# Attention in one encoder layer: the per-block sums over keys folded from 128 to 64 partitions ahead of their transposes

## The chip, the cores and the metric

The kernel runs on one core of a Trainium2 chip. The metric is the device time of one execution in microseconds (us), the median of the runs shown. The core's engines work side by side, each through its own queue of instructions in a fixed order: TensorE (PE, with its weight loads shown as PEld), VectorE (DVE), ScalarE (ACT), GpSimd (POOL) and SyncE (SP), which here issues DMAs.

## What is computed

One layer of a hybrid encoder over 2048 positions of width 1024. A combined projection feeds two groups of heads: a gated linear attention (chunked, in both directions) and a latent attention with softmax over all 2048 keys. Their outputs are joined, projected by a 1024x1024 matrix, added to the scaled input and normalised. The change lies in the softmax attention, whose core is

```python
s = (jnp.einsum('bqhd,bkhd->bhqk', qn, k_nope) + jnp.einsum('bqhr,bkr->bhqk', qr, k_r))
p = jax.nn.softmax(s, axis=-1)
return jnp.einsum('bhqk,bkhv->bqhv', p, v)
```

for 4 heads. What matters for the change is the denominator of the softmax: for each query, the sum over all keys of exp(s - maximum).

## The kernel before

The program has three long stages one after the other: sweeps over the input that make projections, the linear attention and the latent keys and queries (to about 637 us of the profile), the softmax attention (to about 1100 us, its last block running on into the next stage), and the output projection with the normalisation.

The attention works on 16 blocks, each one head and 512 queries (`blocks`, numbered i from 0 to 15). A block has 8 key steps j, each of two tiles of 128 keys. Scores stand transposed: keys on the 128 partitions, the 512 queries along the row. Every product is done in three passes over high and low halves, so that float32 accuracy is kept. The steps of a block, by their functions:

- `scores` (L1512): ten matmuls of 512 columns into a PSUM tile `pS` of two banks; two such tiles take turns. `copy` (L1526, ACT) brings it to SBUF as `s`, and `smax` (L1531, DVE) keeps a running maximum `rm` from PSUM. A tile `pS` is free for the scores two steps later when both have read it.
- `tmax`, `rmax`, `bmax`: four transposes of `rm` (tile `mx`), a reduction along the row, and four more transposes that broadcast the maximum (`mb`).
- `sub` (DVE), `exp` (ACT), `phi` (ACT) and `plo` (POOL): the exponentials and their high and low halves `ph`, `pl`.
- `pv` (L1600): six matmuls that add the step's part to the block's output `o`.
- `acc0`, `acc`: the sums of the exponentials over the key steps. Steps 0, 1, 2, 5 are added in PSUM (`ap`, one buffer) by DVE, after `acc0` on ACT has started it with a copy; steps 3, 4, 6, 7 are added in SBUF (`as`, shown as `acc`, two rows of 512) by POOL.
- `tot` (L1610): DVE joins the two, so that `as[:, 0]` holds for each partition and each query the sum over the 16 key tiles. What is left is the sum over the 128 partitions.
- `tsum` (L1625): four transposes of 128x128 put queries on partitions (tile `sx`, L1629); `rcp` (L1631) adds along the row (L1635) and takes the reciprocal (L1636). `keep` stores it to DRAM for the output stage.
- `oh`, `ol`, `y`, `yc`: the block's output is split, multiplied by the value weights and stored.

The order of all of this on every engine is written out by hand: each step has a place on a common scale (`PLACE`), whole numbers being the score steps; the steps are sorted by place and each engine's instructions are chained in that order. Block i's `tot` is at 8i + 7 + 11.2, which is within block i+2's scores; by then block i+1 is in its exponentials. The last block (15) follows a table of its own and closes during the output projection; block 14's closing steps run among the first products of the output projection.

Lines that the change and the prediction touch: `tot` L1616 and L1617, `tsum` L1629, `rcp` L1635, `acc0` L1585, `copy` L1529, `smax` L1542, `exp` L1570, the split helper L365 (ACT: `ph`, `ofh`) and L371 (POOL and DVE: `pl`, `ofl`), the scores L1520 to L1524.

Of the kernel before, what the change touches and what calls it, by code (L numbers as in the profile page):

```python
# [12 lines left out]
AF = mybir.ActivationFunctionType  # L13
ALU = mybir.AluOpType
AX = mybir.AxisListType
# [12 lines left out]
QB = 512  # L28
# [56 lines left out]
    rmax=1.27,  # L85
    bmax=1.48,
    tot=11.2,
    tsum=12.04,
    rcp=13.55,
    keep=14.21,  # L90
    oh=12.34,
    ol=12.99,
    y=16.55,
    yc=16.9,
# [260 lines left out]
class K:  # L355
# [1130 lines left out]
    def attention(self):  # L1486
        tc, nc = self.tc, self.nc
        mm = nc.tensor.matmul
        V, G, Ac = nc.vector, nc.gpsimd, nc.scalar
        NP = NKT // 2  # L1490
        with ExitStack() as ctx:
# [6 lines left out]
            nb = len(blocks)  # L1498
            stt = [dict(s=[None] * NP) for _ in blocks]
# [110 lines left out]
            def tot(i):  # L1610
                d = stt[i]
                if i == nb - 1:
                    d["as"] = self.keep.tile([P, 2, QB], F32, tag="acc", name=f"acc{i}")
                    V.tensor_copy(d["as"][:, 0], d["ap"])
                    return
                V.tensor_tensor(d["ap"], d["ap"], d["as"][:, 1], ALU.add)  # L1616
                V.tensor_tensor(d["as"][:, 0], d["ap"], d["as"][:, 0], ALU.add)  # L1617

            def close(i, shape, name, other):


                p, tag = other if i == nb - 1 else (pX, "x")
                return p.tile(shape, F32, tag=tag, name=name)

            def tsum(i):  # L1625
                d = stt[i]
                d["x"] = close(i, [P, 4, P], f"sx{i}", (pA, "ap"))
                for e in range(4):
                    nc.tensor.transpose(d["x"][:, e], d["as"][:, 0, e * P:(e + 1) * P], self.ident)  # L1629

            def rcp(i):  # L1631

                d = stt[i]
                rc = op.sm.tile([P, 4], F32, tag="rc", name=f"rc{i}")
                V.tensor_reduce(rc, d["x"], AX.X, ALU.add)  # L1635
                V.reciprocal(rc, rc)  # L1636
                d["rc"] = rc

# [58 lines left out]
            def at(f, i, j=None):  # L1697
                p = PLACE_LAST.get(f, PLACE[f]) if i == nb - 1 else PLACE[f]
                return p[j] if isinstance(p, tuple) else p

            own = (("tot", tot), ("tsum", tsum), ("rcp", rcp), ("keep", keep), ("oh", oh), ("ol", ol), ("y", y), ("yc", yc))
            own_late = tuple(e for e in own if e[1] is not keep)
            for i in range(nb):
                for j in range(NP):
# [81 lines left out]
            for c in range(4, NCH):  # L1786
                with fixed():
                    split(c + 2)
                    load(c + 4)
                    if 4 < c < NCH - 1:  # L1790
                        op.load_res(rest[c + 1])
                    op.product(rest[c])
                    op.finish(rest[c])
                with self.after(*last.values()), fixed():
                    if c == 4:
                        keep(nb - 2)
                    for f in {4: (tot, oh, ol), 5: (tsum, rcp), 7: (turn, y, rows, yc)}.get(c, ()):
                        f(nb - 1)
# [212 lines left out]
```

## Time and profile before

| what | us |
|---|---|
| median of 3 runs (lowest, highest) | 1307.95 (1307.42, 1308.66) |
| the profiled execution | 1308.66 |
| its span, first to last instruction | 1306.3 |
| outside the span | 2.36 |
| TensorE busy in the span | 1280.9 (98%) |
| 637 to 1098 us, the attention: busy PE, POOL, DVE, ACT | 459.1, 407.7, 401.1, 381.2 of 461.0 |
| 1098 to 1145 us: busy PE | 46.0 of 47.0 |
| 1145 to 1306 us, the output projection: busy PE | 150.3 of 161.0 |

Busy time of an engine is the share of the stretch in which one of its instructions ran. Matmuls overlap, so the time that one of them costs is read from the distance between starts, not from its own duration. A line of the timeline gives start, duration from the first start to the last end, engine, line of the code, output and inputs, the count, and in brackets how long the engine had been idle and what released it.

### The profile page before, as it was taken

To read this page: it belongs to the slowest core of one execution; us is meant where nothing else is said; L and a number is where in the kernel's file an instruction comes from. 1 tells how busy PE (TensorE), PEld (TensorE's weight loads), DVE (VectorE), ACT (ScalarE), POOL (GpSimd) and SP (SyncE) were. 2 spreads that over 40 slices of the span, in tenths; PEclk is the share of its full clock that TensorE was granted. 3 is DMA by queue.
4 is the path that set the end of the run, shared out by engine and by line. 5 is a ranking of instruction groups with operands and counts; after the bars stand their busy time and mean duration, and the time that the engine had idled before them with its cause. 6 is when DMAs were issued, how large, how long until landed. Compare 5 with 4: busy or idle time off the path is not lost.

```text
span 1306.3 us, 19979 instructions
## 1 busy us (share of the span) xinstructions
PE 1280.9 (98%) x7081; PEld 1130.9 (87%) x7081; DVE 958.2 (73%) x1712; ACT 812.8 (62%) x1339; POOL 783.6 (60%) x494
## 2 busy tenths in 40 slices
PE   7999999999999999999999999999999999999997
PEld 7999999999989999999788888888888887887786
DVE  6967774645675455555798888888888888377998
ACT  6764656655575656655688878888888888411110
POOL 0143333242457666672298888889999999934441
PEclk9999999999999999999999999999999999999999
DMA  8131313122475565565501111122123110376563
GB/s 285 61 101 54 94 49 91 55 68 79 132 249 170 193 214 181 178 210 170 145 1 41 41 42 41 41 57 65 58 81 97 41 41 12 119 234 175 195 197 109
DMA packets 107820, 145.81 MB, mean 112 GB/s; under 512 B 17251, under 2 KB 62695, under 8 KB 107721
## 3 DMA queue, kind: packets, MB, share of 16 engines
q1 hardware_dynamic: 99128, 142.41, 35.6%
q0 software_dynamic: 672, 2.10, 0.4%
q8 instruction: 56, 0.92, 0.3%
q10 hardware_dynamic: 7920, 0.03, 0.3%
q14 instruction: 44, 0.35, 0.2%
HBM read 94.14 MB, written 50.36 MB: 111 GB/s over the span
## 4 chain that ended last, share of the span: by engine, by line
PE 83%; DMA 4%; DVE 3%; ACT 2%; POOL 1%; issue 1%; SPq 1%; DVEq 0%; POOLq 0%; ACTq 0%
PE pS L1520 4%; PE o L419 4%; PE o L420 4%; PE o L421 4%; PE pS L1522 4%; PE pS L1523 4%; PE pS L1521 4%; PE pS L1524 4%; PE ipa L419 4%; PE ipa L421 4%; PE ipa L420 4%; PE pz L420 2%; PE pz L419 2%; PE pz L421 2%; PE ipg L419 2%; PE ipg L420 2%
## 5 line engine op out<-in xcount | busy, mean ns | idle before, releaser
L371 POOL TENSOR_TENSOR pl<-s,ph 128x1024 fp32r<-128x1024 f32 x128 | 306.5, 2414 | 58.3 <-ACT ph L365 54.5
L1542 DVE TENSOR_TENSOR rm<-pS,rm 128x512 f32<-128x512 f32 x210 | 144.8, 690 | 36.5 <-ACT s L1529 31.2
L1529 ACT ACTIVATE s<-pS 128x1024 f32<-128x1024 f32 x128 | 131.4, 1027 | 60.6 <-PE pS L1524 51.3
L1566 DVE TENSOR_TENSOR s<-s,mb 128x1024 f32<-128x1024 f32 x128 | 151.2, 1213 | 9.5 <-PE mb L1560 9.3
L1029 POOL TENSOR_TENSOR Us<-Us,cw 128x512 f32<-128x512 f32 x16 | 18.5, 1157 | 227.2 <-DVE Us L1027 175.3
L365 ACT ACTIVATE ph<-s 128x1024 fp32r<-128x1024 f32 x128 | 135.2, 1057 | 17.1 <-PE o L421 16.5
L1570 ACT ACTIVATE s<-s 128x1024 f32<-128x1024 f32 x128 | 131.4, 1050 | 13.7 <-DVE s L1566 13.7
L419 PE MATMUL ipa<-wah,xah 128*128 128x384 f32 (+1 forms) x384 | 131.1, 342 | 6.7 <-ACT wah L365 6.7
L421 PE MATMUL ipa<-wah,xal 128*128 128x384 f32 (+1 forms) x384 | 125.5, 327 | 0.0
L420 PE MATMUL ipa<-wal,xah 128*128 128x384 f32 (+1 forms) x384 | 125.2, 326 | 0.0
L1520 PE MATMUL pS<-qh,ckvT_h 128*128 128x512 f32 x256 | 102.6, 401 | 0.8 <-DVE rm L1542 0.4
L419 PE MATMUL o<-ph,vh 128*128 128x512 f32 x256 | 101.0, 395 | 0.0
L421 PE MATMUL o<-ph,vl 128*128 128x512 f32 x256 | 99.8, 390 | 0.0
L1522 PE MATMUL pS<-qh,ckvT_l 128*128 128x512 f32 x256 | 99.8, 390 | 0.0
L1523 PE MATMUL pS<-rh,krs 128*128 128x512 f32 x256 | 99.8, 390 | 0.0
L1524 PE MATMUL pS<-rl,krs 128*128 128x512 f32 x256 | 99.7, 389 | 0.0
L1521 PE MATMUL pS<-ql,ckvT_h 128*128 128x512 f32 x256 | 99.7, 389 | 0.0
L420 PE MATMUL o<-pl,vh 128*128 128x512 f32 x256 | 99.7, 389 | 0.0
L1593 DVE TENSOR_TENSOR ap<-ap,s 128x512 f32<-128x512 f32 x120 | 83.0, 692 | 2.7 <-ACT s L1570 0.7
L371 POOL TENSOR_TENSOR ol<-of,oh 128x512 fp32r<-128x512 f32 x32 | 42.9, 1343 | 66.9 <-ACT oh L365 66.9
L419 PEld LDWEIGHTS ipa<-wah,xah 128*128 128x128 f32 x384 | 73.7, 192 | 7.9 <-ACT wah L365 7.0
L419 PE MATMUL pz<-xch,wzh 128*128 128x256 f32 x256 | 74.8, 292 | 0.0
(325 smaller groups left out, 3858.0 us busy)
## 6 DMA issues: line engine op xcount, KB each, us to landing
xcf<-xT_dram SPq DMA_DIRECT2D x16, 512.0 KB, 4.9
xr<-x_dram SPq DMA_DIRECT2D x16, 512.0 KB, 6.6
out_dram<-rr SPq DMA_DIRECT2D x32, 256.0 KB, 2.0
xaf<-xT_dram SPq DMA_DIRECT2D x14, 512.0 KB, 4.2
oib<-oi_s SPq DMA_DIRECT2D x16, 256.0 KB, 4.4
qdb<-qd_s SPq DMA_DIRECT2D x16, 256.0 KB, 4.6
SU<-su_s SPq DMA_DIRECT2D x16, 256.0 KB, 4.9
ub<-u_s SPq DMA_DIRECT2D x16, 256.0 KB, 4.7
```

The lines of the kernel that those rows point to most:

```text
L365: return nc.scalar.activation(dst, src, AF.Copy).ins
L371: return e.tensor_tensor(dst, src, hi.bitcast(F32), ALU.subtract).ins
L419: mm(out, ah, bh, start=start, stop=False)
L420: mm(out, ah, bl, start=False, stop=False)
L421: mm(out, al, bh, start=False, stop=stop)
L1520: mm(ps[:, e], kh, qh, start=True, stop=False)
L1521: mm(ps[:, e], kh, ql, start=False, stop=False)
L1522: mm(ps[:, e], kl, qh, start=False, stop=False)
L1523: mm(ps[:, e], kr, rh, start=False, stop=False)
L1524: mm(ps[:, e], kr, rl, start=False, stop=True)
L1542: V.tensor_tensor(d["rm"], src[:, e], d["rm"], ALU.max)
L1566: V.tensor_tensor(s, s, d["mb"][:, None, :].to_broadcast([P, 2, QB]), ALU.subtract)
```

## The change

Ahead of the transposes, the 128 partitions are folded to 64. `tot` now leaves the joined sum in PSUM (`ap`). A new step `own_half` on ACT (two copies of 64 partitions by 256 queries) puts partitions 0 to 63 of queries 0 to 255 and partitions 64 to 127 of queries 256 to 511 into `as[:, 0, :256]`. A new step `fold` on DVE (two additions of 64 by 256) adds the other 64 partitions of the same queries, which it reads from PSUM across the partition halves. `as[:, 0, :256]` then holds two sums of 64 partitions for every pair of queries, one above the other, and `tsum` needs two transposes in place of four; `rcp` adds rows of 64 in place of rows of 128. The last block keeps the former way. The places are 11.7 for `own_half`, 11.95 for `fold` and 12.37 for `tsum` (12.04 before).

```diff
     tot=11.2,
-    tsum=12.04,
+    half=11.7,
+    fold=11.95,
+    tsum=12.37,
...
-                V.tensor_tensor(d["ap"], d["ap"], d["as"][:, 1], ALU.add)
-                V.tensor_tensor(d["as"][:, 0], d["ap"], d["as"][:, 0], ALU.add)
+                for e in range(2):
+                    V.tensor_tensor(d["ap"], d["ap"], d["as"][:, e], ALU.add)
+
+            halves = [(slice(64 * e, 64 * e + 64), slice(64 - 64 * e, 128 - 64 * e), slice(e * QB // 2, (e + 1) * QB // 2))
+                      for e in range(2)]
+
+            def own_half(i):
+                d = stt[i]
+                for own_p, _, qs in halves:
+                    Ac.activation(d["as"][own_p, 0, :QB // 2], d["ap"][own_p, qs], AF.Copy)
+
+            def fold(i):
+                d = stt[i]
+                for own_p, other_p, qs in halves:
+                    h = d["as"][own_p, 0, :QB // 2]
+                    V.tensor_tensor(h, d["ap"][other_p, qs], h, ALU.add)
...
-                for e in range(4):
+                for e in range(4 if i == nb - 1 else 2):
                     nc.tensor.transpose(d["x"][:, e], d["as"][:, 0, e * P:(e + 1) * P], self.ident)
...
-                V.tensor_reduce(rc, d["x"], AX.X, ALU.add)
+                if i == nb - 1:
+                    V.tensor_reduce(rc, d["x"], AX.X, ALU.add)
+                else:
+                    V.tensor_reduce(rc.rearrange("p (e j) -> p j e", e=2),
+                                    d["x"][:, 0:2].rearrange("p j (e k) -> p j e k", e=2), AX.X, ALU.add)
...
-            own = (("tot", tot), ("tsum", tsum), ("rcp", rcp), ("keep", keep), ("oh", oh), ("ol", ol), ("y", y), ("yc", yc))
+            own = (("tot", tot), ("half", own_half), ("fold", fold), ("tsum", tsum), ("rcp", rcp), ("keep", keep), ("oh", oh), ("ol", ol), ("y", y), ("yc", yc))
```

What stands in a row on an engine is shown for the end of block 6, which falls into block 8's scores; the other blocks up to 13 read the same. A name's first number in a row, where it has two, is the key step; the last is the program's own count. Here is DVE before, from `tot` to the reduction of `rcp`: `rm` and `pS` belong to block 8, `s` and `mb` to block 7, `acc` to block 6.

```order
L1616 TENSOR_TENSOR ap_9658<-ap_9658,acc_9788 128x512
L1617 TENSOR_TENSOR acc_9788<-ap_9658,acc_9788 128x512
L1542 TENSOR_TENSOR rm_9881<-pS_1_9870,rm_9881 128x512 x2
L1566 TENSOR_TENSOR s_3_9685<-s_3_9685,mb_9857 128x1024
L1542 TENSOR_TENSOR rm_9881<-pS_2_9899,rm_9881 128x512 x2
L1566 TENSOR_TENSOR s_4_9731<-s_4_9731,mb_9857 128x1024
L1566 TENSOR_TENSOR s_5_9760<-s_5_9760,mb_9857 128x1024
L371 TENSOR_TENSOR ofl_9965<-o_9720,ofh_9955 128x512
L1542 TENSOR_TENSOR rm_9881<-pS_3_9935,rm_9881 128x512 x2
L1593 TENSOR_TENSOR ap_9932<-ap_9932,s_0_9592 128x512
L1635 TENSOR_REDUCE rc_10004<-sx_9946 128x4
```

The same stretch of DVE after the change:

```order
L1619 TENSOR_TENSOR ap_9670<-ap_9670,acc_9800 128x512 x2
L1544 TENSOR_TENSOR rm_9893<-pS_1_9882,rm_9893 128x512 x2
L1568 TENSOR_TENSOR s_3_9697<-s_3_9697,mb_9869 128x1024
L1633 TENSOR_TENSOR acc_9800<-ap_9670,acc_9800 64x256 x2
L1544 TENSOR_TENSOR rm_9893<-pS_2_9911,rm_9893 128x512 x2
L1568 TENSOR_TENSOR s_4_9743<-s_4_9743,mb_9869 128x1024
L1568 TENSOR_TENSOR s_5_9772<-s_5_9772,mb_9869 128x1024
L373 TENSOR_TENSOR ofl_9979<-o_9732,ofh_9966 128x512
L1544 TENSOR_TENSOR rm_9893<-pS_3_9951,rm_9893 128x512 x2
L1595 TENSOR_TENSOR ap_9946<-ap_9946,s_0_9602 128x512
L1654 TENSOR_REDUCE rc_10018<-sx_9968 128x2x2
```

Nothing changes its place; the two additions of `fold` are put in between a `sub` of block 7 and the maximum of block 8's step 2. On ACT, the copies of `own_half` come between block 7's `ph` of step 0 and block 8's copy of step 2, after the change:

```order
L1572 ACTIVATE s_0_9602<-s_0_9602 128x1024
L367 ACTIVATE ph_0_9934<-s_0_9602 128x1024
L1627 ACTIVATE acc_9800<-ap_9670 64x256 x2
L1531 ACTIVATE s_2_9944<-pS_2_9911 128x1024
L1587 ACTIVATE ap_9946<-s_0_9602 128x512
L1572 ACTIVATE s_1_9633<-s_1_9633 128x1024
L367 ACTIVATE ofh_9966<-o_9732 128x512
L367 ACTIVATE ph_1_9971<-s_1_9633 128x1024
L1531 ACTIVATE s_3_9975<-pS_3_9951 128x1024
```

Before, the same rows stood there without the third; `ap_9946` is block 7's `acc0`, which writes the single buffer `ap` that `fold` reads two rows of work earlier. On PE the transposes `sx` stay between block 8's scores of step 3 and of step 4, two in place of four.

## The prediction

> **What bounds the kernel now.** I read the head of the page first, then the attention's stretches by engine, then PE's timeline around the transposes that the change halves. All these rows are of the kernel before; the first pair is from the page, the third from the table of stretches (PE, PEld, DVE, ACT, POOL busy, then granted clock, DMA share and GB/s) for one period of the attention, from the end of block 6's sum to the end of block 7's.
>
> ```profile
> span 1306.3 us, 19979 instructions
> PE 1280.9 (98%) x7081; PEld 1130.9 (87%) x7081; DVE 958.2 (73%) x1712; ACT 812.8 (62%) x1339; POOL 783.6 (60%) x494
> ...
> 858.77:889.89 31.12, 31.12 (x145) 25.79 (x144) 27.00 (x38) 26.18 (x29) 27.65 (x12) 1.00 0.03 9
> ```
>
> PE is busy for all of the 31.12 us at the full granted clock, while DVE, ACT and POOL have 3.5 to 5 us free in each period. A busy PE may still be a slow one, so the spacing of its matmuls is what counts. PE's timeline, with the scores of block 8 around block 6's transposes:
>
> ```profile
> 864.39 0.39 PE L1524 MATMUL pS<-rl,krs 128*128 128x512 f32 x1
> 864.62 0.60 PE L1629 MATMUL sx<-ident,acc 128*128 128x128 f32 x4
> 864.98 0.48 PE L1520 MATMUL pS<-qh,ckvT_h 128*128 128x512 f32 x1
> 865.29 0.39 PE L1521 MATMUL pS<-ql,ckvT_h 128*128 128x512 f32 x1
> ...
> 868.70 0.39 PE L1520 MATMUL pS<-qh,ckvT_h 128*128 128x512 f32 x1
> 870.97 0.39 PE L419 MATMUL o<-ph,vh 128*128 128x512 f32 x1
> ```
>
> Matmuls of 512 columns start every 0.23 us (864.39 to 864.62 here), with no gap before the transposes. So in the attention PE's own list of instructions is the time, and whatever is taken from it counts in full, as long as no wait opens.
>
> **What the change takes from PE.** One transpose lasts 272 ns by the group of its line:
>
> ```profile
> L1629 PE MATMUL sx<-ident,acc 128*128 128x128 f32 x64 | 9.6, 272 | 0.0
> ```
>
> Four take 0.60 us from the first start to the last end, so three spacings are 0.60 - 0.272 = 0.328, or 0.109 us each. The whole group costs 864.62 to 865.29 less one ordinary spacing, 0.67 - 0.23 = 0.44 us, four times 0.11: the price is linear in the count. Two transposes less are 0.218 us a block, and 15 of the 16 blocks change: 3.27 us. The bounds from the same rows: if only the way to the next start counts, 0.36 / 4 = 0.09 us a transpose, 2.7 us in all; with the slow matmul behind them spread over the four, 0.11 each, 3.4 us. I take 3.27, since neighbours in a row are what is removed.
>
> The Trainium skill has a lower price: "TensorE: Matmul & The Clock Gate", section "Back-to-back issue gap", gives about 81 ns for a pair of weight load and matmul of 128 columns in a sustained stream. By it the sum would be 30 x 0.081 = 2.4 us, an estimate from that page, which would not be told from no change; the 0.109 us measured here stands against it.
>
> **What the change adds.** Prices by the nearest rows, first ACT then DVE:
>
> ```profile
> L1267 ACT ACTIVATE sqm<-ipm 128x256 f32<-128x256 f32 x16 | 6.1, 384 | 12.6 <-DVE rope L1469 9.6 <-PE ipm L421 3.0
> L365 ACT ACTIVATE qbh<-qd 64x512 fp32r<-64x512 f32 x32 | 20.2, 631 | 8.2 <-DVE qd L936 7.7
> L1465 DVE TENSOR_TENSOR qrf<-pqr,cos 128x256 f32<-128x256 f32 x16 | 6.7, 419 | 5.5 <-PE pqr L421 5.5
> L371 DVE TENSOR_TENSOR qbl<-qd,qbh 64x512 fp32r<-64x512 f32 x32 | 23.6, 737 | 2.9 <-ACT qbh L365 2.3
> ```
>
> 64 partitions of 512 cost as much as full rows of 512 below, so the row length decides, and I take the rows of 256 from PSUM. Neighbours overlap by about 0.1 us, so `own_half` is 2 x 0.384 - 0.1 = 0.67 us of ACT (at most 1.16, by 64x512) and `fold` 2 x 0.419 - 0.1 = 0.74 us of DVE (at most 1.37). `rcp`'s reduction halves its row, 0.68 to about 0.42, and gives 0.26 back. The second addition of `tot` keeps its form and only writes elsewhere. None of it is on PE; the question is whom it makes late. ACT and DVE in the period above, before the change, and POOL's row that follows ACT's `ph` of 863.04:
>
> ```profile
> 858.27 1.06 ACT L365 ACTIVATE ph<-s 128x1024 fp32r<-128x1024 f32 x1
> 859.89 1.03 ACT L1529 ACTIVATE s<-pS 128x1024 f32<-128x1024 f32 x1 [0.56 <-PE pS L1524]
> 860.81 0.59 ACT L1585 ACTIVATE ap<-s 128x512 f32<-128x512 f32 x1
> 861.33 1.05 ACT L1570 ACTIVATE s<-s 128x1024 f32<-128x1024 f32 x1
> 862.55 0.60 ACT L365 ACTIVATE ofh<-o 128x512 fp32r<-128x512 f32 x1 [0.17 <-PE o L421]
> 863.04 1.05 ACT L365 ACTIVATE ph<-s 128x1024 fp32r<-128x1024 f32 x1
> 864.88 1.03 ACT L1529 ACTIVATE s<-pS 128x1024 f32<-128x1024 f32 x1 [0.78 <-PE pS L1524]
> ```
> ```profile
> 858.08 0.69 DVE L1617 TENSOR_TENSOR acc<-ap,acc 128x512 f32<-128x512 f32 x1
> 860.01 1.21 DVE L1566 TENSOR_TENSOR s<-s,mb 128x1024 f32<-128x1024 f32 x1
> 861.14 1.41 DVE L1542 TENSOR_TENSOR rm<-pS,rm 128x512 f32<-128x512 f32 x2
> 865.94 1.42 DVE L1542 TENSOR_TENSOR rm<-pS,rm 128x512 f32<-128x512 f32 x2 [0.53 <-ACT s L1529]
> 867.87 0.68 DVE L1635 TENSOR_REDUCE rc<-sx 128x4 f32<-128x512 f32 x1
> ```
> ```profile
> 864.23 2.41 POOL L371 TENSOR_TENSOR pl<-s,ph 128x1024 fp32r<-128x1024 f32 x1 [2.35 <-ACT ph L365]
> ```
>
> - `own_half` waits for `tot`, done at 858.77, and ACT is free at 859.33 and idle for 0.56 us: the copy behind it moves from 859.89 to about 860.0.
> - `fold` starts where the maximum stood, 861.14, and ends near 861.9. It pushes block 8's step 2 maximum to 861.9 to 863.3. The scores at 864.98 wait for that one; their lead shrinks from 2.4 to 1.7 us.
> - The new wait: `acc0` of block 7 writes `ap`, which `fold` still reads, so ACT stands from 861.0 to 861.9 and `acc0` moves from 860.81 to 861.95. Behind it `exp`, `ofh`, `ph` and the next copy are queued. The idle times 0.17 and 0.78 take 0.95 of the 1.14 us, so the copy of 864.88 comes about 0.2 us late, and so does the maximum of 865.94 (DVE's own 0.74 less its idle 0.53 is also 0.2). The scores at 868.70 reuse that tile: free at 867.36 before, a lead of 1.34 us, now about 1.1. The shorter reduction then makes DVE whole.
> - POOL's `pl` of 864.23 waits for `ph`, about 1 us late, and ends at 867.6 instead of 866.64; the `pv` that reads it starts at 870.97, still 3.3 us later.
> - `sx` itself had 5.85 us from `tot`'s end to 864.62; `fold` ends 2.7 us ahead of it.
>
> With the upper prices `fold` ends at 862.5, `acc0` is 1.7 us late, the copy of 864.88 0.75 and the lead of 868.70 0.5 us; still no wait on PE.
>
> Block 14 closes outside this pattern:
>
> ```profile
> 1107.56 1.21 DVE L1566 TENSOR_TENSOR s<-s,mb 128x1024 f32<-128x1024 f32 x1
> 1107.68 0.60 ACT L1585 ACTIVATE ap<-s 128x512 f32<-128x512 f32 x1 [0.45 <-DVE acc L1617]
> 1111.19 0.60 ACT L365 ACTIVATE ofh<-o 128x512 fp32r<-128x512 f32 x1 [1.92 <-PE o L421]
> 1110.99 0.60 PE L1629 MATMUL sx<-ident,acc 128*128 128x128 f32 x4
> ```
>
> `fold` follows the `sub` and ends near 1109.4, 1.5 us ahead of `sx`; `acc0` slips by 1.8 us into ACT's 1.92 us of idle time. Covered, with little to spare.
>
> **Whether the tail passes it on.** PE is not gapless after the attention. The chain that ended last (start, length, what):
>
> ```profile
> 1142.01 0.03 PE o L421
> 1142.04 3.60 DMA xr<-x_dram
> ...
> 1208.38 0.70 DVE rr L1926
> 1209.08 0.14 issue
> 1209.22 0.47 PE pmb L419
> ```
> ```profile
> 1205.90:1209.67 3.77, 0.62 (x3) 0.44 (x3) 1.25 (x2) 0.00 (x0) 0.05 (x1) 1.00 0.98 307
> 1209.67:1213.08 3.41, 3.41 (x10) 2.62 (x9) 3.31 (x8) 0.92 (x3) 0.47 (x1) 0.50 0.76 237
> ```
>
> PE stands for about 3.2 us until 1209.22, behind a chain of transfers, and then runs 3.41 us at half clock. But that chain was released at 1142.04 by PE itself, by the last block's products. An attention that ends 3.27 us earlier starts the chain as much earlier. So the tail moves along.
>
> **The sum.** 1308.66 - 3.27 = 1305.4 for the profiled execution (2.36 us of it outside the span). The median lies 0.71 below that run: 1304.7, or -0.25%. Changes within 0.2%, 2.6 us, count as no change, about what a measurement of this kernel can tell; so the forecast lies just outside.
>
> **The rivals.**
>
> - *The gain is partly lost.* The tail's stall depends on how transfers fall, and the half clock behind it lasted 3.41 us, in which 10 matmuls took the time of 15: 1.7 us. A longer stall could bring a second such stretch, +1.7, for 1306.4; without any it would be 1303.0. The lowest price of a transpose, 0.09, gives 1305.3. For it: the three runs before already spread over 1.24 us. Against it: the chain's start moves with PE, and the spacing inside the group is plain. The Trainium skill, "TensorE: Matmul & The Clock Gate", section "What's actually happening", says that the clock follows a free-running window of 3413 ns; this trace's 3.41 us agree. By that rule a shift of 3.27 us neither keeps nor removes the half-clock stretch for sure.
> - *Slower: PE waits for ACT at the scores of 868.70.* The place is `acc0` behind `fold`. It decides once ACT is late by more than 0.95 + 1.34 = 2.3 us, against my 1.14; each period then costs PE the excess, 14 times, and from 0.23 us of excess the gain is gone. At an excess of 0.5 us it is +7.0 - 3.27, 1311.7. Against it: even the upper prices reach 1.7. For it: three engines hand on in a row (DVE, ACT, DVE, ACT), and a semaphore hop of 0.14 us, as at 1209.08, stands in each.
> - *Nothing is gained, since weight loads hide transposes.* Then 1307.9; the spacing of 0.109 with a matmul behind each speaks against it, so I give it no chance beside the first rival's.
>
> **How the numbers follow.** Whole saving 0.64 (1304.0 to 1305.3); whole saving and no half-clock stretch 0.05 (near 1303.0); partly lost 0.21 (1305.3 to 1307.5); slower 0.10 (near 1311.7). The predicted time is the first case's. Faster by over 0.2% is 0.64 + 0.05 = 0.69, within it 0.21, slower 0.10. The range 1303.0 to 1306.8 leaves out the slower case and the top of the partly lost one, under 2 in 10; the two prices of a transpose lie inside it.
>
> **What would show it.** Right: `sx` in pairs, about 0.38 us from the first start to the last end; periods of 30.90 us in place of 31.12; no idle time on PE in the attention; `acc0` waiting up to 1 us for DVE; the output's chain starting near 1138.8. Wrong: PE waiting for `rm`, for `fold` or for `pl` in each block; a stall before `pmb` well over 3 us; or a pair of transposes that costs over 0.3 us.

## The result and the profile after

The changed kernel takes 1304.42 us (median of 14 runs, 1302.11 to 1306.13), the kernel before took 1308.14 us beside it (median of 14). The ratio is 0.9972, with a 95% interval from 0.9965 to 0.9979: 0.28% faster, or 3.7 us. The profiled execution of the changed kernel took 1305.11 us, that of before 1308.66. From the head of its page:

```profile
span 1303.1 us, 20008 instructions
PE 1276.8 (98%) x7051; PEld 1126.2 (86%) x7051; DVE 970.7 (74%) x1742; ACT 821.2 (63%) x1369; POOL 783.8 (60%) x494
```

PE has 30 matmuls fewer, DVE and ACT 30 instructions more each. PE's timeline of the changed kernel (start, length, then the operation) at block 6's transposes:

```profile
863.85 0.39 PE L1526 MATMUL pS<-rl,krs 128*128 128x512 f32 x1
864.08 0.38 PE L1645 MATMUL sx<-ident,acc 128*128 128x128 f32 x2
864.22 0.48 PE L1522 MATMUL pS<-qh,ckvT_h 128*128 128x512 f32 x1
864.53 0.39 PE L1523 MATMUL pS<-ql,ckvT_h 128*128 128x512 f32 x1
...
867.73 0.39 PE L423 MATMUL o<-ph,vl 128*128 128x512 f32 x1
867.96 0.39 PE L1522 MATMUL pS<-qh,ckvT_h 128*128 128x512 f32 x1
...
894.96 0.38 PE L1645 MATMUL sx<-ident,acc 128*128 128x128 f32 x2
```

There are pairs now, 0.38 us from the first start to the last end. From the first transpose to the second matmul behind the group it is 0.45 us, where 0.23 would be one ordinary spacing: the pair costs 0.22. The period, from one `sx` to the next, is 894.96 - 864.08 = 30.88 us. Over blocks 0 to 13 it is 30.889 us on average, before 31.102: 0.213 us less. The matmuls before the scores of 867.96 keep their spacing of 0.23, so no gap has opened. PE's waits (what it waited for: us in total, times, longest) in the attention and behind it, of before and then of after, show no new one either (the two lines not shown are the same in both):

```profile
PE pmb L419 <- DVE rr L1926: 3.1, 1, 3.1
PE mx L1548 <- DVE rm L1542: 1.3, 2, 1.0
...
PE pS L1520 <- DVE rm L1542: 0.4, 1, 0.4
```
```profile
PE pmb L421 <- DVE rr L1946: 3.0, 1, 3.0
PE mx L1550 <- DVE rm L1544: 1.0, 2, 0.7
...
PE pS L1522 <- DVE rm L1544: 0.4, 1, 0.4
```

ACT and DVE of the changed kernel in the same period:

```profile
858.69 0.75 ACT L1627 ACTIVATE acc<-ap 64x256 f32<-64x256 f32 x2
859.47 1.03 ACT L1531 ACTIVATE s<-pS 128x1024 f32<-128x1024 f32 x1
861.66 0.60 ACT L1587 ACTIVATE ap<-s 128x512 f32<-128x512 f32 x1 [1.17 <-DVE acc L1633]
...
864.57 1.02 ACT L1531 ACTIVATE s<-pS 128x1024 f32<-128x1024 f32 x1
```
```profile
860.71 0.86 DVE L1633 TENSOR_TENSOR acc<-ap,acc 64x256 f32<-64x256 f32 x2
861.60 1.42 DVE L1544 TENSOR_TENSOR rm<-pS,rm 128x512 f32<-128x512 f32 x2
...
865.79 1.41 DVE L1544 TENSOR_TENSOR rm<-pS,rm 128x512 f32<-128x512 f32 x2
...
867.72 0.41 DVE L1654 TENSOR_REDUCE rc<-sx 128x4 f32<-128x256 f32 x1
```

`acc0` (L1587) now stands 1.17 us for the fold, and ACT's idle time ahead of the copy of 864.57 is gone. The maximum of 865.79 ends at 867.20; the scores that need its tile start at 867.96, a lead of 0.76 us where it was 1.34.

So the time went where the change took it. Followed through the two profiled executions:

| place on PE | before | after | difference |
|---|---|---|---|
| first `sx` (block 0) | 678.00 | 678.74 | +0.74 |
| `sx` of block 13 | 1082.33 | 1080.30 | -2.03 |
| `sx` of block 14 | 1110.99 | 1108.50 | -2.49 |
| `sx` of block 15 | 1182.88 | 1180.15 | -2.73 |
| first `pmb` behind the tail's stall | 1209.22 | 1206.32 | -2.90 |
| span | 1306.3 | 1303.1 | -3.2 |

Of the 0.74 us, 0.69 were there at PE's first wait of the attention (637.90 before, 638.59 after), behind work that the change does not touch; the first `sx` of the other kernels below that have it at this place stands anywhere from 677.50 to 678.32. From block 0 to block 13 the gain is 2.77 us, 13 x 0.213. The rest of the path gives it on and adds a few tenths: the two waits of `mx`, one of which lies between blocks 13 and 14, are 0.3 us shorter in all.

The time outside the span moved as well: 2.36 us in the profiled execution before, 2.0 in that of after and within 0.1 us of it in all 14 runs. It is 2.0 in every kernel below that has the half copy and the fold (1.75 in the one with a second fold), and 2.3 in the two with the transposes alone and in the middle of the 56 runs of the kernel before beside the experiments. So about 0.3 of the 3.7 us lies outside the span, and no run shows what it comes from.

### The profile page after: what moved, and what is told of

It is laid out like the page before. It is cut to its first block, busy times and chain, and to the rows that moved or that the text cites. A ratio compares the mean times of both kernels' runs of the same rounds, so it can differ in the third digit from the quotient of the medians.

```text
span 1303.1 us, 20008 instructions
## 1 busy us (share of the span) xinstructions
PE 1276.8 (98%) x7051; PEld 1126.2 (86%) x7051; DVE 970.7 (74%) x1742; ACT 821.2 (63%) x1369; POOL 783.8 (60%) x494
## 4 chain that ended last, share of the span: by engine, by line
PE 82%; DVE 4%; DMA 4%; ACT 3%; POOL 2%; issue 1%; SPq 0%; DVEq 0%; ACTq 0%; POOLq 0%
PE o L421 4%; PE o L422 4%; PE o L423 4%; PE pS L1522 4%; PE pS L1524 4%; PE pS L1523 4%; PE pS L1525 4%; PE pS L1526 4%; PE ipa L421 4%; PE ipa L423 4%; PE ipa L422 4%; PE pz L422 2%; PE pz L423 2%; PE pz L421 2%; PE ipg L421 2%; PE ipg L422 2%
```

## The experiments

The theory: PE's list of instructions is the time in the attention, each transpose costs it about 0.11 us, and the added half copy and fold lie beside PE's work and use up only margin. The rivals: a transpose's price is hidden or other than that; the added work costs something, and the gain would be larger without it. All were timed in five rounds beside the kernel before, which took 1306.32 us in the first group of four, 1305.62 in the second and 1306.33 in the group of three. The expectations count their absolute times from some 1308 us, so the ratios are what to compare. A period is the average over blocks 0 to 13, as above, and in the first group the middle one of the 13.

**Each half of the change alone, first try.** Of four kernels three held a substitute that I thought neutral: a constant operation of DVE in place of `rcp`'s reciprocal.

```diff
-                V.reciprocal(rc, rc)
+                V.tensor_scalar(rc, rc, 1.0, None, ALU.add)   # blocks 0 to 14
```

Two transposes without the half copy and the fold:

> Two transposes a block in place of four, with neither own_half nor fold (tot as before the change; half of each sum is left out, and blocks 0 to 14 add a constant where the reciprocal stood, one instruction of the same shape). Theory (TensorE's own list is the time, the added work of ScalarE and VectorE is covered): the same as the changed kernel, about 1304.6, pairs of 0.38 us, periods of 30.89 us. Rival (the added work costs part of the gain): 1.5 us or more below the changed kernel, 1303 or less. Rival (the gain comes from elsewhere, the tail for one): close to 1308.

Measured: 1303.42 us, ratio 0.9979 (0.9970 to 0.9988), period 30.91 us. The half copy and fold with all four transposes:

> own_half and fold as in the change, but four transposes and the full reduction (the sums are then wrong, and a constant is added where the reciprocal stood). Theory: the kernel before, 1308.0 within 0.7, periods of 31.1 us, no wait of TensorE in the attention. Rival (the added work costs something that two transposes hide): over 1309.

Measured: 1311.82 us, ratio 1.0045 (1.0032 to 1.0059), period 31.58. One transpose in place of two:

> One transpose a block in place of two (the second 128 queries are left out, the reduction takes four parts of the one; a constant in place of the reciprocal). Theory (0.109 us a transpose, linear down to one): 15 x 0.108 = 1.6 us less than the changed kernel, 1302.8, periods of 30.78 us. Rival (81 ns a transpose): 1303.2. Rival (the last transpose of a group carries the fixed cost of the slow matmul behind it, so that it cannot be saved and nothing is won): 1304.4.

Measured: 1311.33 us, ratio 1.0041 (1.0028 to 1.0053), period 31.58, though PE has less to do than in the changed kernel. Both slow ones wait at the scores one step later than those I had watched, here in the run with one transpose:

```profile
876.01 0.39 PE L423 MATMUL o<-ph,vl 128*128 128x512 f32 x1
876.92 0.47 PE L1522 MATMUL pS<-qh,ckvT_h 128*128 128x512 f32 x1 [0.52 <-DVE rm L1544]
```

The substitute is the cause they share. The rows of DVE and then POOL in the run with one transpose, and the groups of that instruction in the runs with the fold alone and with the pairs alone:

```profile
871.41 1.58 DVE L1658 TENSOR_SCALAR rc<-rc 128x4 f32<-128x4 f32 x1
```
```profile
868.19 4.78 POOL L373 TENSOR_TENSOR pl<-s,ph 128x1024 fp32r<-128x1024 f32 x2 [3.46 <-ACT ph L367]
```
```profile
L1659 DVE TENSOR_SCALAR rc<-rc 128x4 f32<-128x4 f32 x15 | 16.6, 1110 | 0.5
```
```profile
L1659 DVE TENSOR_SCALAR rc<-rc 128x4 f32<-128x4 f32 x15 | 16.4, 1094 | 0.5
```

Four elements a row take 1.1 to 1.6 us in all blocks but the last that has it (0.17), where the reciprocal takes 0.18. So these runs added about 1 us of DVE ahead of the next step's maximum, together with the fold, and they say nothing on the fold by itself. With the pairs alone, where DVE has no fold to do, the same 1.1 us were covered.

**The fold later on DVE.** One number of the order changes, the fold goes behind the maximum of step 2, so that `acc0` waits longer.

```diff
-    fold=11.95,
+    fold=12.25,
```

> Only fold moves, from before block i+2's maximum of step 2 to behind it (place 12.25). Theory: acc0, and with it ScalarE's exp, ofh, ph and copy of step 3, come about 1.3 us later than in the changed kernel, which is 0.5 us more than the lead of the scores that reuse that tile; TensorE waits about 0.4 to 0.5 us for the maximum of step 3 in each of 14 periods: 1310 to 1311.5. Rival (the leads read from the trace are not what decides, or the lateness is taken up elsewhere): no change, about 1304.4.

Measured: 1311.62 us, ratio 1.0047 (1.0035 to 1.006), period 31.58. ACT, DVE and PE of that run, around block 6's close, and PE's wait of the whole run:

```profile
867.00 0.60 ACT L1587 ACTIVATE ap<-s 128x512 f32<-128x512 f32 x1 [2.49 <-DVE acc L1633]
...
869.91 1.02 ACT L1531 ACTIVATE s<-pS 128x1024 f32<-128x1024 f32 x1
```
```profile
866.05 0.85 DVE L1633 TENSOR_TENSOR acc<-ap,acc 64x256 f32<-64x256 f32 x2
...
870.96 1.42 DVE L1544 TENSOR_TENSOR rm<-pS,rm 128x512 f32<-128x512 f32 x2 [1.07 <-ACT s L1531]
```
```profile
871.76 0.39 PE L423 MATMUL o<-ph,vl 128*128 128x512 f32 x1
872.52 0.47 PE L1522 MATMUL pS<-qh,ckvT_h 128*128 128x512 f32 x1 [0.37 <-DVE rm L1544]
```
```profile
PE pS L1522 <- DVE rm L1544: 6.4, 15, 0.9
```

This is the slower rival of the prediction, made to happen: `acc0` waits 2.49 us for the fold in place of 1.17, the copy behind it comes late, DVE waits 1.07 us for the copy, and PE stands for the maximum, once a period (0.76 us from start to start in place of 0.23). The period is 0.69 us longer than the changed kernel's. The wait is 0.53 of it, a little more than the 0.4 to 0.5 expected; the matmul behind the delayed one starts 0.31 us after it in place of 0.23, another 0.08; the last 0.08 are spread over many spacings.

**The halves of the change again, with the reciprocal kept.** Two transposes alone (the reduction reads each of the two tiles twice):

```diff
# in the kernel before
-                for e in range(4):
+                for e in range(4 if i == nb - 1 else 2):
```

> The kernel before with one edit: two transposes a block in place of four, and a reduction that still reads 512 elements, the two tiles twice (the second 256 queries of a block get the first's sums). Reciprocal kept. Theory: 15 x 0.218 = 3.3 us less than the kernel before, as the changed kernel. Rival (the added work of the change costs part of the gain): 4 us or more below the kernel before.

Measured: 1302.58 us, ratio 0.9976 (0.9966 to 0.9985), period 30.888 us. That is the change's own period, 30.889. The half copy and fold with four transposes (of two pieces, each twice):

```diff
# in the changed kernel
-                for e in range(4 if i == nb - 1 else 2):
-                    nc.tensor.transpose(d["x"][:, e], d["as"][:, 0, e * P:(e + 1) * P], self.ident)
+                for e in range(4):
+                    s = e if i == nb - 1 else e % 2
+                    nc.tensor.transpose(d["x"][:, e], d["as"][:, 0, s * P:(s + 1) * P], self.ident)
```

> The changed kernel with four transposes, the two of the change done twice, and a reduction that adds both (a block's sums then come out wrong), reciprocal kept. Theory: the added work is covered, and the slow result of the first attempt came from the constant's addition, which took 1.1 us in place of 0.18: the kernel before within 0.7 us, periods of 31.1 us, no wait of TensorE. Rival (0.26 us more of reduction on VectorE already uncovers a wait): 2.5 us or more above the kernel before.

Measured: 1304.91 us, ratio 0.9997 (0.9987 to 1.0006), period 31.124 us. The reduction in this kernel stayed the changed kernel's short one, so this is the change without its gain on PE and nothing else. And one transpose in place of two, whose tile the reduction reads twice:

> The changed kernel with one transpose a block in place of two; the reduction has the shape of the change and reads the one tile twice (half of the queries get other sums), reciprocal kept. Theory (0.108 us a transpose down to the last but one): 1.6 us below the changed kernel, that is 5.0 below the kernel before, periods of 30.78 us. Rival (81 ns a transpose): 1.2 below the changed kernel. Rival (TensorE, 0.1 us a period faster, meets the maximum of step 3 or 4): periods of 30.9 us or more.

Measured: 1299.96 us, ratio 0.9956 (0.9941 to 0.9971), period 30.788 us, with no new wait on PE.

These three settle the account. The added work alone changes nothing that can be measured; the transposes alone give the change's whole gain of the period (of the time 0.24% in place of 0.28%, within the intervals); a third transpose less gives another step of the same size. By the periods, one transpose is worth (31.124 - 30.889) / 2 = 0.117 us with the fold, (31.102 - 30.888) / 2 = 0.107 without it, and 30.889 - 30.788 = 0.101 from two to one. The first two prices differ because the two kernels with four transposes do, 31.124 and 31.102, with the same list on PE.

**Whose margin it is.** Three more kernels test it. One moves the fold and `acc0`, one `acc0` alone (behind ACT's copy of step 3, where it does not wait for the fold), and one lengthens the reduction. First the late fold with a late `acc0`:

```diff
-    acc0=10.78,
+    acc0=11.75,
-    fold=11.95,
+    fold=12.25,
```

> The late fold of the third experiment, and acc0 behind ScalarE's copy of step 3 (place 11.75; block 15 keeps 10.78), so that exp, ofh, ph and the copy no longer stand behind the wait for fold. Theory (the late fold cost 7 us through acc0's wait alone): the changed kernel's time, periods of 30.89 us, no wait of TensorE. Rival (the late fold costs through VectorE, whose later work it pushes): periods of 31.5 us and some 5 us above the kernel before, as with the late fold.

Measured: 1303.08 us, ratio 0.9979 (0.9969 to 0.9989), period 30.910 us: the loss of the late fold is gone. ACT in that run:

```profile
861.54 0.60 ACT L368 ACTIVATE ofh<-o 128x512 fp32r<-128x512 f32 x1 [0.57 <-PE o L424]
...
863.87 1.03 ACT L1532 ACTIVATE s<-pS 128x1024 f32<-128x1024 f32 x1 [0.78 <-PE pS L1527]
864.79 0.60 ACT L1588 ACTIVATE ap<-s 128x512 f32<-128x512 f32 x1
```

`acc0` is taken without a wait, and ACT's idle 0.78 us ahead of the copy is back. So the late fold cost through `acc0`'s place in ACT's queue, not through DVE. Now the late `acc0` alone, with the fold where the change has it:

> The changed kernel with one number of the order changed: acc0 of the next block stands after exp on ACT (as in the run with both the fold and acc0 late), the fold stays where the change has it. If the wait of acc0 for the fold (1.17 us of ACT) eats only margin, the time is that of the changed kernel (period 30.89, ratio to the kernel before 0.997 to 0.998), but ACT's wait of 1.17 us is gone and the lead of the scores of step 5 goes from 0.76 back to about 1.3 us. Rival: that wait costs PE something that its list of waits doesn't show, and the period falls below 30.85.

Measured: 1301.66 us, ratio 0.9969 (0.9958 to 0.998), period 30.91 us. The time is the changed kernel's, as expected; the lead is not. DVE's maximum and PE's scores in that run:

```profile
860.40 0.86 DVE L1634 TENSOR_TENSOR acc<-ap,acc 64x256 f32<-64x256 f32 x2
861.28 1.42 DVE L1545 TENSOR_TENSOR rm<-pS,rm 128x512 f32<-128x512 f32 x2
862.62 2.34 DVE L1569 TENSOR_TENSOR s<-s,mb 128x1024 f32<-128x1024 f32 x2
864.88 0.68 DVE L374 TENSOR_TENSOR ofl<-o,ofh 128x512 fp32r<-128x512 f32 x1
865.48 1.41 DVE L1545 TENSOR_TENSOR rm<-pS,rm 128x512 f32<-128x512 f32 x2
```
```profile
867.67 0.39 PE L1523 MATMUL pS<-qh,ckvT_h 128*128 128x512 f32 x1
```

The maximum ends at 866.89, 0.78 us ahead of the scores, as in the changed kernel (0.76), with ACT's wait gone. DVE works from the fold to that maximum without a gap: in the changed kernel the lead is set by DVE's own work, and `acc0`'s 1.17 us lie within it. Last, the reduction at its old length:

```diff
-                                    d["x"][:, 0:2].rearrange("p j (e k) -> p j e k", e=2), AX.X, ALU.add)
+                                    d["x"][:, 0:2].rearrange("p j (e k) -> p j e k", e=2)[:, :, :, None].to_broadcast([P, 2, 2, 2, 64]), AX.XY, ALU.add)
```

> The changed kernel, but the reduction of the pair reads every element twice (512 columns instead of 256, about 0.68 instead of 0.41 us), so that its result, and with it the output, is off by a factor of two. It tests the sentence that the shorter reduction makes DVE whole. If that holds as a need, DVE is 0.26 us later after each reduction, the scores behind lose as much of their lead, and where the lead was under 0.26 us PE waits: period 31.1 us or more, ratio to the kernel before 1.000 to 1.005. Rival: the margins behind the reduction are larger than that, and the period stays at 30.89 us, ratio 0.997 to 0.998.

Measured: 1301.92 us, ratio 0.9968 (0.9956 to 0.998), period 30.911 us. The rival holds: the reduction took 0.68 us, and PE waited for nothing new. The margin behind the reduction is more than 0.27 us; the two kernels with the substitute, which put some 1.3 us more on DVE there than the change does (for the fold alone 0.27 of reduction and 1.0 of the substitute, for one transpose 1.4 less 0.13), were over it.

**The step carried further.** A second half copy and a second fold, to 32 partitions, in blocks 0 to 13, and one transpose; its result is complete. The order was changed with it: `acc0` moves to place 12.6, the first two sums of the block, the transpose and what follows it later too.

```diff
+            def own_quarter(i):
+                d = stt[i]
+                for own_p, _, qs in quarters:
+                    Ac.activation(d["as"][own_p, 0, :P], d["ap"][own_p, qs], AF.Copy)
...
+                for own_p, other_p, qs in quarters:
+                    h = d["as"][own_p, 0, :P]
+                    V.tensor_tensor(h if i == nb - 2 else d["ap"][own_p, qs], d["ap"][other_p, qs], h, ALU.add)
...
-                for e in range(4 if i == nb - 1 else 2):
+                for e in range({nb - 1: 4, nb - 2: 2}.get(i, 1)):
```

> The step carried further: in blocks 0 to 13 a second copy on ACT and a second addition on DVE fold the sums from 64 to 32 partitions, and one transpose a block is left instead of two; block 14 keeps the pair and block 15 its four. acc0 stands later in the order, so that it doesn't wait for the fold. If the price of a transpose (0.10 to 0.117 us) is taken from PE and the two added steps lie beside PE's work, the period falls from 30.89 to about 30.78 us, 14 x 0.11 = 1.5 us in all: ratio to the kernel before near 0.996. Rival: DVE has about 1.1 us more to do in each period, and the maximum that frees the tile of the next scores comes late: PE waits for rm once a period, the period goes to 31.5 us, and the kernel is slower than the one before (ratio near 1.004).

Measured: 1312.21 us, ratio 1.004 (1.0027 to 1.0052), period 31.45 us: the rival. ACT, DVE and PE of that run:

```profile
865.61 1.11 ACT L1645 ACTIVATE acc<-ap 32x128 f32<-32x128 f32 x4 [0.26 <-DVE ap L1637]
...
872.46 0.60 ACT L1591 ACTIVATE ap<-s 128x512 f32<-128x512 f32 x1 [0.36 <-DVE acc L1651]
874.46 1.03 ACT L1535 ACTIVATE s<-pS 128x1024 f32<-128x1024 f32 x1 [1.40 <-DVE ap L1599]
```
```profile
871.18 1.19 DVE L1651 TENSOR_TENSOR acc<-ap,acc 32x128 f32<-32x128 f32 x4
```
```profile
876.51 0.39 PE L427 MATMUL o<-ph,vl 128*128 128x512 f32 x1
877.28 0.47 PE L1526 MATMUL pS<-qh,ckvT_h 128*128 128x512 f32 x1 [0.38 <-DVE rm L1548]
```

Four additions of 128 columns cost DVE 1.19 us, more than the two of 256 (0.86). DVE has no gap from the second fold at 871.18 to the maximum behind ACT's copy; `acc0` waits for the second fold, the sums stand behind it, ACT's copy waits 1.40 us for the sums, the maximum comes late, and PE stands 0.54 us a period (0.77 less 0.23) where a transpose less would give 0.1. The same transpose left out without this work gave 30.788 us. So this order has no room for the work that replaces the transpose; whether another order has, was not tried. No version with a complete result that is measurably faster than the changed kernel came out of these runs.

What stays open: the late fold, the fold alone and the one transpose with the substitute all end at a period of 31.58 us. For the latter two, whose lists on PE differ by three transposes, the equal period says that PE's list no longer sets it; why the late fold, with another wait, comes to the same figure was not found. Nor was the cause of the 0.02 us between the periods 30.889 and 30.91 of kernels with the same work on PE (the pair 31.102 and 31.124 is like it): in the traces it is no wait, but a few nanoseconds at a time in the spacing of matmuls.

## Why the prediction was right

- **PE's list is the time in the attention.** Right. The period fell by the transposes' price, in the change and in the pair without the fold alike, and PE's list of waits gained nothing.
- **The price of a transpose.** Taken at 0.109 us; the periods give 0.101 to 0.117. The pair costs 0.22 us, the foretold 0.218. (The upper bound was added up wrongly: 30 x 0.11 is 3.3 us, not 3.4.) The Trainium skill's price for a pair of weight load and matmul of 128 columns ("TensorE: Matmul & The Clock Gate", "Back-to-back issue gap", about 81 ns) is under all three of these measurements; the 2.4 us that it gave is outside the interval of the measured gain, 2.7 to 4.6 us (0.21 to 0.35% of 1308.14). The sum of 3.27 us lies within, and by the periods it is 15 x 0.213 = 3.2 us.
- **What the sum left out.** It took the 2.36 us outside the span as given. They fell to 2.0, and the attention of the profiled execution began 0.7 us later than before. That 1304.7 came so near to the 1304.42 measured is in part luck; the fall of the period is not.
- **The added work is covered.** Right: the half copy and fold with four transposes run at 0.9997 of the time before. Both sizes were too low, 0.75 us for the half copy (0.67 foretold) and 0.86 for the fold (0.74). The pieces are 0.37 and 0.42 us each, as foretold; what was missing is that the two pieces do not overlap by the 0.1 us that rows of all 128 partitions showed.
- **The new wait.** `acc0` stands 1.17 us, foretold 0.95 (861.0 to 861.9). Mechanism and place are right.
- **POOL's `pl`.** It comes late with `ph`, as foretold, by 1.1 us: 0.73 us behind `sx` (864.81 less 864.08), where it began 0.39 ahead of it. PE does not wait for it.

```profile
864.81 4.78 POOL L373 TENSOR_TENSOR pl<-s,ph 128x1024 fp32r<-128x1024 f32 x2 [3.46 <-ACT ph L367]
```

- **The lead of the next scores.** The term that missed: 0.76 us, not 1.1. I had let the maximum come 0.2 us late, by either of two reckonings. With the fold's real length, DVE's own reckoning is 0.86 - 0.53 = 0.33. And the scores themselves come 0.2 us earlier than before, counted from `sx`: 867.96 - 864.08 = 3.88 us, before 868.70 - 864.62 = 4.08. A shorter list on PE takes its gain out of the lead of everyone who works for the next item in it. 1.34 - 0.33 - 0.2 = 0.81, close to the 0.76 measured. The late `acc0` showed further that DVE's share, not ACT's wait, is what counts in the changed kernel.
- **The shorter reduction makes DVE whole.** True of DVE's sum, but not needed: with the long one the time is the same.
- **Block 14.** The fold was to end 1.5 us ahead of `sx`, and `acc0`'s delay to fit into ACT's idle 1.92 us. Here is ACT of the changed kernel, and DVE's fold:

```profile
1107.24 0.60 ACT L1587 ACTIVATE ap<-s 128x512 f32<-128x512 f32 x1 [1.28 <-DVE acc L1633]
1108.95 0.60 ACT L367 ACTIVATE ofh<-o 128x512 fp32r<-128x512 f32 x1
```
```profile
1106.29 0.86 DVE L1633 TENSOR_TENSOR acc<-ap,acc 64x256 f32<-64x256 f32 x2
```

  The fold ends at 1107.15, 1.35 us ahead of `sx` at 1108.50. `ofh` no longer waits: counted from `sx` it starts 0.45 us behind, before 0.20. So the idle time was used up to the end, and a little more; nothing on PE shows it.

- **The tail moves along.** The chain's transfer of `x` begins at 1139.31 (foretold near 1138.8, with 0.74 us lost ahead of the attention), the stall before `pmb` is 3.0 us, and a half-clock stretch follows it, as before. From the windows of two runs with the same period and the same work on PE, the late `acc0` and then the long reduction (PE, PEld, DVE, ACT, POOL busy, granted clock, DMA share, GB/s):

```profile
1207.00:1209.00 2.00, 2.00 (x7) 1.52 (x6) 1.93 (x5) 0.93 (x3) 0.08 (x1) 0.50 0.78 234
```
```profile
1207.00:1209.00 2.00, 2.00 (x11) 1.65 (x10) 2.00 (x3) 0.75 (x3) 1.14 (x1) 1.00 0.72 272
```

  One execution had the half-clock stretch in its tail and the other had none, with spans of 1302.6 and 1299.9 us. PE at half clock in the first of them:

```profile
1207.23 0.63 PE L422 MATMUL pmb<-woh,oh 128*128 128x512 f32 x1
1207.66 0.63 PE L423 MATMUL pmb<-wol,oh 128*128 128x512 f32 x1
```

  Its matmuls start 0.43 us apart in place of 0.23, eight in the 3.41 us, which costs 1.6 us. The prediction's 1.7 is near it, though not by its own count: two of its ten matmuls only reach into the stretch, and five of 0.23 would be 1.15. The 2.7 us between the two spans add up: 0.73 was there at `sx` of block 15, the stall before `pmb` is 0.33 longer (2.32 and 1.99), and the stretch is 1.6.

  The 13 profiled executions divide in the same way: six have the stretch, with stalls of 2.2 to 3.9 us before `pmb`, and seven have none, with 1.1 to 2.0. The granted clock, averaged over the span, is 0.996 to 0.997 in the six and 0.998 to 0.999 in the seven. By that mark 11 of the 14 runs of the changed kernel had it, and 12 of the 56 runs of the kernel before beside the experiments, with medians of 1307.5 us with it and 1305.6 without. For the 14 runs of before beside the result the mark is on record for the profiled one alone, which has it. So the size of the partly lost gain was right as a price, but it is paid or spared from run to run, and the median shows no loss.

- **The slower rival** was put at over 2.3 us of delay on ACT, against 1.14 foretold. `acc0` waiting 2.49 us brought it about, at the foretold place and for the foretold reason. That its 1311.62 us look like the 1311.7 worked out for half a microsecond a period is luck: 1311.7 counted from 1307.95, the kernel before took 1306.32 beside this run, and each period lost 0.69 us. The hop between two engines, put at 0.14 us, is 0.09 from the fold to `acc0` (861.57 to 861.66). At 1.17 us it does not occur.

## What to carry to other kernels

Where one engine's list of instructions runs gapless, an instruction taken from it is worth its spacing among its neighbours (0.11 us here), not its duration (0.27), and work moved to other engines is free only up to the lead of the next item that the bounding engine needs; write that lead down first, and take the gain itself off it. The same trade made once more (one transpose less for 1.2 us of VectorE) went from 0.3% faster to 0.4% slower, so the second step of a good idea is to be priced afresh. And where work waits in an in-order queue, moving what is queued behind it is often enough: the late fold lost 0.7% against the changed kernel with `acc0` behind it, and nothing that can be measured once `acc0` was moved.

## What the runs showed of the hardware

Not expected was the constant operation on DVE. In all three kernels that have it, it ran 1.05 to 1.6 us in blocks 0 to 13, while POOL was in a TENSOR_TENSOR, and its end came 24 to 34 ns after POOL's instruction ended, 42 times of 42. In block 14, where POOL was idle, it took 0.17 us. The reciprocal of the same 128x4 tile takes 0.18 us with POOL's `pl` running beside it, and the fold, whose inputs lie in PSUM and SBUF, keeps its 0.42 us an addition with `pl` running through most of it. The Trainium skill has a rule that fits: "SBUF — State Buffer", section "Who interferes with whom", says that `tensor_scalar` can enter a mode that uses both of VectorE's ports, one of which is GpSimd's, that the pair is locked for a whole instruction, and that whoever comes second waits it out; an instruction with at most one input in SBUF outside that mode does not contend. The times of the constant operation and of the fold agree with both halves of the rule; in which mode an instruction ran, and why the reciprocal is spared, no run here shows. For experiments it means that a stand-in for a tiny operation has to be looked up in the trace before its run is read: this one cost up to 1.4 us a block and turned two of the first four runs into answers to another question.
